# A two-layer hybrid decoder in one kernel: scaled rows and transposes for the norms, column blocks for the NSA compression

## The chip, the cores and the metric

One NeuronCore of a Trainium2 chip. The metric is the device time of one execution in microseconds (us). The kernel before was run three times: median 2697.93 us, from 2696.49 to 2704.11. The trace comes from a further, profiled execution.

## The reference, cut to what matters

Two layers, each a token mixer and a gated MLP, both between RMS norms with an adaptive shift, scale and gate. Sequence 256, width 2048, one batch, float32. Only what the change touches:

```python
h = rms_norm(x, norm_pre_mix[l]) * (1.0 + sc1) + sh1          # pre_norm; the same before the MLP
y = token_mixing(h, ...)                                      # four head groups, then w_out
x = x + g1 * rms_norm(y, norm_post_mix[l])

# inside token_mixing, each group's output is normalised: MLA, S5, NSA
o = concat([rms_norm(o_a, gn_mla), rms_norm(o_b, gn_s5), rms_norm(o_c, gn_nsa), o_d])

# NSA compression: 15 blocks of 32 rows, stride 16, of k and of v
h = gelu((xb + pos_emb).reshape(B, N, L * D) @ w1); k_cmp = h @ w2

# S5: a diagonal complex scan over time per group, 32 groups of 16 channels, 64 states
x_t = lam * x_{t-1} + B u_t ;  y_t = Re(C x_t) + d * u_t
```

MLA's two inputs (384 and 256 wide) have an RMS norm too.

## The kernel before, in words

Everything runs in one program that is written down once; a scheduler puts each engine's instructions into a fixed order by priorities, and the engines keep to it. Whatever waits holds up all that stands behind it on its engine.

**The weight stream.** The large products read float32 weight tiles of 128x1024 (`wload`, line 406, one transfer of 512 KB each). ScalarE rounds a tile to a high part `wh` (L423) and VectorE takes the rest `wl` (L424), both with raised priority; TensorE makes three products of each pair (`mm3`), named `mm<-ht,wh`, `mm<-ht,wl` and so on, where `ht` holds the split activations. Everything else that TensorE does goes into PSUM banks `mx` from two pools of two banks, "lanes" 0 and 1; with `lane = None` allocations alternate between the lanes. A bank is handed out in the order of the program, so a step that takes banks of a lane waits for the earlier step in that lane.

**Plain float32 products.** Products that don't go through the split stand in the trace as two weight loads and two matmuls each, one per pass. A transpose stands there once.

**pre_norm** (L577 on) runs three times: before the MLP of layer 0, before layer 1's mixer, before the MLP of layer 1. `residual` (L679) computes the row statistics on VectorE and builds two diagonal matrices, `set_diag` (L569; L573 on VectorE). `x` (two halves of 128 rows, `tt`) is updated in four column blocks `j` (L701), the first two before the products, the last two after the first part of pre_norm. TensorE multiplies each 128x128 block of `x` by the diagonal, which transposes and scales it at once (32 products per norm); ScalarE adds scale and shift (L597), and the result is split into `ht` (L599, L600). The first four of eight steps `k2` are written ahead of the weight stream, the rest between its tiles.

**norm_T** (L770) normalises a group's output that lies transposed: ScalarE squares it (L777), TensorE adds up the squares over partitions with a column of ones, one product for each 128 columns, VectorE computes the reciprocal root, TensorE spreads it over the partitions, VectorE applies it (L784). It runs five times per layer: S5, MLA q, MLA kv, MLA out, NSA out.

**nsa_compress** (L971) computes, for k and for v, `st` (18 columns: 16 blocks and two position vectors for each of 16 row offsets) times `w1`, which comes in four tiles `rawm` of 512 KB (two buffers, L454, moderate priority). All 16 products add up in the same 18 PSUM partitions of one bank, 256 columns wide. The sum is copied, transposed in two pieces, and goes through gelu and `w2`. It uses lane 1.

**s5** (L1537) uses lane 0 and works on four quarters (half, parity): eight products for `V` (64 rows of the array: the parity's half), the twists, scans and back-twists on VectorE (L1542, L1577), and twelve products for `y`, whose output goes to 64 partitions (again the parity's half). `s5_tables` prepares matrices, with products in blocks of 64 output partitions.

In `mixers` the order is: S5, the two token-major products (`gemm_a`), gates, `nsa_compress`, the remaining weight products for GDN, the two GDN halves in lockstep, one per lane, then MLA and NSA in lockstep, then `w_out`.

Of the kernel before, what the change touches and what calls it, by code (L numbers as in the profile page):

```python
# [12 lines left out]
F32 = mybir.dt.float32  # L13
# [3 lines left out]
AF = mybir.ActivationFunctionType  # L17
# [175 lines left out]
class Ker:  # L193
# [102 lines left out]
    def constants(self):  # L296
# [38 lines left out]
        self.diag = t([P, 2, P], F32, "diag")  # L335

        self.cm01 = t([P, 2, 32], F32, "cm01")
        self.cmadd = t([P, 2, 32], F32, "cmadd")
# [227 lines left out]
        self.rsqrt(v, y, self.sm(ss.shape[-1], "ra"))  # L566
        return y

    def set_diag(self, ss):  # L569

        r = self.rsqrt_cols(ss)
        for tt in range(2):
            i = self.nc.vector.tensor_scalar(self.diag[:, tt], self.ident, r[:, tt:tt + 1], 1.0 / RSC,  # L573
                                             op0=ALU.mult, op1=ALU.mult)
        return i

    def pre_norm(self, l, which):  # L577

        nc = self.nc
        for k2 in range(KT // 2):  # L580
            if k2 in (2, 4, 6):
                yield
            ps = self.mx()
            for i in range(2):
                k = 2 * k2 + i
                for tt in range(2):
                    self.mm(ps[:, i * 256 + tt * P:i * 256 + (tt + 1) * P], self.x[:, tt, k * P:(k + 1) * P],
                            self.diag[:, tt], True, True)
# [12 lines left out]
            if k2 == 0 and self.add_rest is not None:  # L601
                self.turn_ins = (i,) + self.turn_ins[1:]
                self.add_rest(i)
                self.add_rest = None

    def row_scale(self):
# [72 lines left out]
    def residual(self, sums, zs, done):  # L679

        nc = self.nc
        tot = self.small.tile([P, 3, 2], F32, name="bt", tag="bt", bufs=1)
        nc.vector.tensor_reduce(tot, sums, axis=AX.X, op=ALU.add)
        r = self.rsqrt_cols(tot[:, 0])
        sxx = self.x_stats()
        t = self.sm(2, "ct")
        for tt in range(2):
            nc.vector.scalar_tensor_tensor(t[:, tt:tt + 1], tot[:, 1, tt:tt + 1], r[:, tt:tt + 1], tot[:, 2, tt:tt + 1],
                                           op0=ALU.mult, op1=ALU.add)
        for tt in range(2):  # L690
            nc.vector.scalar_tensor_tensor(t[:, tt:tt + 1], t[:, tt:tt + 1], r[:, tt:tt + 1], sxx[:, tt:tt + 1],
                                           op0=ALU.mult, op1=ALU.add)
        d = self.set_diag(t)
# [9 lines left out]
        add(range(2), d)  # L703
        self.add_rest = lambda i: add(range(2, 4), i)

    def new_squares(self):
        with self.after(*self.norm_ins):
# [62 lines left out]
    def norm_T(self, scr, chunks, banks, n, gains, outs):  # L770

        nc = self.nc
        ss = self.mx(2)
        i, m = 0, 2 * len(chunks)
        for bi, (b, w) in enumerate(banks):
            sq = scr[:, bi % 2 * 512:bi % 2 * 512 + w]
            nc.scalar.activation(sq, b, AF.Square)  # L777
            for j in range(w // P):
                self.mm(ss[:, j % 2:j % 2 + 1], sq[:, j * P:(j + 1) * P], self.ones[:, 0:1], i == 0, i == m - 1)
                i += 1  # L780
# [192 lines left out]
    def nsa_compress(self, l, r, kvt, kT, kc, vb):  # L973
# [13 lines left out]
        for nm, src in (("k", kcT), ("v", vT)):  # L987
            w2 = r(P)
            nc.sync.dma_start(w2, I["nsa_w2_" + nm][l])
            st = r(16, 18)  # L990
            nc.vector.tensor_copy(st[:, :, 0:16], src.rearrange("p (m q) -> p q m", q=16))
            nc.vector.tensor_copy(st[:, :, 16:18], self.vs(l, "pos_" + nm).rearrange("p (q h) -> p q h", h=2))
            acc = self.mx(256)
            for q0 in range(0, 16, 4):
                raw = self.mload(I["nsa_w1_" + nm][l, q0 // 4])
                for q in range(4):
                    self.mm(acc[:18], st[:, q0 + q], raw[:, q * 256:(q + 1) * 256], q0 + q == 0, q0 + q == 15)
            ab = r(256)[:18]
            nc.scalar.copy(ab, acc[:18])
# [388 lines left out]
    def s5_tables(self, l, q, gs):  # L1388
# [97 lines left out]
        for half in range(2):  # L1486
# [2 lines left out]
            place(((bbr, bbi), (bbr, bbi)), half)  # L1489
            ps = self.mx(256).rearrange("p (q n) -> p q n", q=4)  # L1490
            for qd in range(4):
                for e in range(2):
                    for ri in range(2):
# [44 lines left out]
    def s5(self, l, r, Uc, oT):  # L1538
# [6 lines left out]
        t1, t2 = (wz[:, i * 516:(i + 1) * 516].rearrange("p (e n) -> p e n", e=4) for i in range(2))  # L1545
# [5 lines left out]
        a1, a2 = t1[:, :, 1:], t2[:, :, 1:]  # L1551
        for t in (t1, t2):
            nc.gpsimd.memset(t[:, :, 0:1], 0.0)
        for qr in range(4):

            half, par = qr // 2, qr % 2
            quads = range(4 * half, 4 * half + 4)
            o = 64 * par
            es = slice(8 * half + par, 8 * half + 8, 2)
            Er, Ei = E[:, 0, es], E[:, 1, es]  # L1560
            V = []
            for ri in range(2):
                ps = self.mx().rearrange("p (e n) -> p e n", e=4)
                for e, qd in enumerate(quads):
                    self.mm(ps[:, e], G[o:o + 64, qd, ri], Uc[o:o + 64, qd], True, True)
                V.append(ps)

            TTm(a1, V[0], Er, mul)
            TTm(a2, V[1], Ei, mul)
            TTm(zr, a1, a2, add)  # L1570
            TTm(a1, V[1], Er, mul)
            TTm(a2, V[0], Ei, mul)
            TTm(zi, a1, a2, sub)
            for z in (zr, zi):
                for e, qd in enumerate(quads):
                    d0 = self.s5m2[:, l, 2 * qd + par:2 * qd + par + 1].to_broadcast([P, P])
                    nc.vector.tensor_tensor_scan(z[:, e], d0, z[:, e], 0.0, mul, add)  # L1577
            TTm(a1, zr, Er, mul)
            TTm(a2, zi, Ei, mul)
            TTm(a1, a1, a2, sub)  # L1580
            TTm(zr, zr, Ei, mul)
            TTm(zi, zi, Er, mul)
            TTm(a2, zr, zi, add)
            y = self.mx().rearrange("p (q n) -> p q n", q=4)
            for e, qd in enumerate(quads):
                yy = y[o:o + 64, e]
                self.mm(yy, To[o:o + 64, qd], Uc[o:o + 64, qd], True, False)
                for ri, t in enumerate((t1, t2)):
                    self.mm(yy, H[:, 2 * qd + par, ri], t[:, e, 0:P], False, ri == 1)
            for h in range(2):  # L1590
                for s in range(2):
                    of = 64 * h + 32 * par
                    nc.scalar.activation(yv[of:of + 32, 2 * half:2 * half + 2, :, s], y[o + 32 * s:o + 32 * s + 32, h::2],  # L1593
                                         AF.Gelu_apprx_tanh)
# [33 lines left out]
    def mixers(self, l, first):  # L1628
# [301 lines left out]
```

## Time and profile before

| | |
|---|---|
| median of three runs | 2697.93 us |
| the profiled execution | 2690.51 us |
| its span, first to last instruction | 2688.7 us |
| TensorE busy | 96% of the span |
| VectorE busy | 71% |
| ScalarE busy | 47% |
| DMA, mean over the span | 231 GB/s |
| granted TensorE clock, mean | 0.977 |

A matmul's duration in the trace includes the time in which it travels through the array, and neighbours overlap in it. The time that it takes from its neighbours is the distance between two starts: of a row with n matmuls of one kind that took T in all, each lasting d, it is (T − d) / (n − 1).

### The profile page before, as it was taken

To read this page: it belongs to the slowest core of one execution; us is meant where nothing else is said; L and a number is where in the kernel's file an instruction comes from. 1 tells how busy PE (TensorE), PEld (TensorE's weight loads), DVE (VectorE), ACT (ScalarE), POOL (GpSimd) and SP (SyncE) were. 2 spreads that over 40 slices of the span, in tenths; PEclk is the share of its full clock that TensorE was granted. 3 is DMA by queue.
4 is the path that set the end of the run, shared out by engine and by line. 5 is a ranking of instruction groups with operands and counts; after the bars stand their busy time and mean duration, and the time that the engine had idled before them with its cause. 6 is when DMAs were issued, how large, how long until landed. Compare 5 with 4: busy or idle time off the path is not lost. (4 is left out here: it accounts for less than half of the span.)

```text
span 2688.7 us, 44484 instructions
## 1 busy us (share of the span) xinstructions
PE 2570.3 (96%) x17604; PEld 2285.4 (85%) x17604; DVE 1908.3 (71%) x3014; ACT 1260.1 (47%) x2004; POOL 10.2 (0%) x22
## 2 busy tenths in 40 slices
PE   7879999898999999999989999989899999999998
PEld 4568788677999999988868888978899999998886
DVE  5568888688787778766978889474777655555555
ACT  3344463556454444444545446454544444444443
POOL 0000000000000000000000000000000000000000
PEclk9979999898999999999999999999999999999999
DMA  8866666676888888866767578255587655555554
GB/s 344 313 209 200 227 239 231 233 277 222 292 284 288 292 290 293 287 228 235 249 220 239 165 251 274 98 193 173 191 278 275 206 187 181 183 185 186 184 189 148
DMA packets 171264, 620.89 MB, mean 231 GB/s; under 512 B 19440, under 2 KB 20272, under 8 KB 169520
## 3 DMA queue, kind: packets, MB, share of 16 engines
q1 hardware_dynamic: 170048, 617.00, 67.0%
q8 instruction: 138, 2.26, 0.3%
q10 hardware_dynamic: 1008, 1.06, 0.1%
q14 instruction: 70, 0.57, 0.1%
HBM read 613.75 MB, written 4.23 MB: 230 GB/s over the span
## 5 line engine op out<-in xcount | busy, mean ns | idle before, releaser
L228 PE MATMUL mm<-ht,wh 128*128 128x256 f32 x7168 | 1311.2, 283 | 6.8 <-ACT ht L423 5.8
L423 ACT CAST wh<-raw 128x1024 fp32r<-128x1024 f32 (+1 forms) x740 | 771.6, 1044 | 965.0 <-PE mm L228 792.1
L424 DVE TENSOR_TENSOR wl<-raw,wh 128x1024 fp32r<-128x1024 f32 (+1 forms) x740 | 895.9, 1213 | 380.2 <-ACT wh L423 377.1
L228 PEld LDWEIGHTS mm<-ht,wh 128*128 128x128 f32 x7168 | 1112.7, 189 | 22.9 <-issue 8.4
L228 PE MATMUL mm<-ht,wl 128*128 128x256 f32 x3584 | 1017.1, 284 | 2.7 <-DVE wl L424 2.7
L228 PEld LDWEIGHTS mm<-ht,wl 128*128 128x128 f32 x3584 | 674.5, 188 | 10.4 <-DVE wl L424 6.3
L228 PE MATMUL mm<-wh,ht 128*128 128x512 f32 (+1 forms) x1600 | 510.8, 396 | 8.6 <-DVE ry L256 3.9
L462 DVE SCALAR_TENSOR_TENSOR acc<-rawa,condc,acc 128x1024 f32<-128x1024 f32 x300 | 384.3, 1281 | 165.4 <-DMA rawa<-in_w_ada_dram 163.0
L228 PEld LDWEIGHTS mm<-wh,ht 128*128 128x128 f32 x1600 | 302.7, 190 | 73.2 <-ACT gth L1377 4.3
L228 PE MATMUL mm<-wl,ht 128*128 128x512 f32 (+1 forms) x800 | 317.2, 396 | 0.6 <-DVE wl L424 0.6
L228 PE MATMUL mx<-arena 128*128 128x128 f32 (+9 forms) x1576 | 228.1, 318 | 15.5 <-DVE gea L1151 9.7
L228 PE MATMUL mx<-wh,ht 128*128 128x512 f32 x704 | 222.3, 396 | 0.0
L228 PEld LDWEIGHTS mx<-arena 128*128 128x128 f32 (+5 forms) x1576 | 161.1, 168 | 59.0 <-issue 20.5
L228 PEld LDWEIGHTS mm<-wl,ht 128*128 128x128 f32 x800 | 152.4, 190 | 31.7 <-DVE wl L424 1.2
L228 PEld LDWEIGHTS mx<-wh,ht 128*128 128x128 f32 x704 | 132.6, 188 | 32.3
L228 PE MATMUL mx<-wl,ht 128*128 128x512 f32 x352 | 139.6, 397 | 0.0
L424 DVE TENSOR_TENSOR ht<-arena,ht 128x1024 fp32r<-128x1024 f32 x52 | 63.6, 1223 | 41.1 <-ACT ht L423 40.8
L1758 DVE SCALAR_TENSOR_TENSOR arena<-mm,vec,arena 128x255 f32<-128x255 f32 (+1 forms) x176 | 78.3, 476 | 6.7 <-ACT arena L1756 5.8
L423 ACT CAST ht<-arena 128x1024 fp32r<-128x1024 f32 x52 | 54.2, 1050 | 56.7 <-PE mm L228 31.3
L228 PEld LDWEIGHTS mx<-wl,ht 128*128 128x128 f32 x352 | 66.3, 188 | 16.5 <-DVE wl L424 0.3
L232 PE MATMUL mx<-ident,arena 128*128 128x128 f32 (+1 forms) x328 | 59.4, 292 | 21.5 <-ACT arena L826 13.7
L232 PEld LDWEIGHTS mx<-ident,arena 128*128 128x128 f32 (+1 forms) x328 | 39.5, 147 | 40.2 <-ACT arena L826 17.4
(314 smaller groups left out, 1520.4 us busy)
## 6 DMA issues: line engine op xcount, KB each, us to landing
raw<-in_ffn_w_in_dram SPq DMA_DIRECT2D x352, 512.0 KB, 4.2
rawa<-in_w_ada_dram SPq DMA_DIRECT2D x330, 512.0 KB, 5.1
raw<-in_ffn_w_out_dram SPq DMA_DIRECT2D x176, 512.0 KB, 4.3
raw<-in_w_in_dram SPq DMA_DIRECT2D x116, 512.0 KB, 4.5
raw<-in_w_out_dram SPq DMA_DIRECT2D x64, 512.0 KB, 4.3
arena<-in_w_ada_dram SPq DMA_DIRECT2D x36, 512.0 KB, 8.0
raw<-in_w_in_dram SPq DMA_DIRECT2D x32, 426.0 KB, 4.0
rawm<-in_w_ada_dram SPq DMA_DIRECT2D x9, 512.0 KB, 9.6
```

Source lines behind the costliest of these rows:

```text
L228: self.nc.tensor.matmul(out, lhsT=lhsT, rhs=rhs, start=start, stop=stop)
L232: self.nc.tensor.transpose(out, in_, self.ident[:k, :k])
L423: self.nc.scalar.copy(hi.bitcast(F32R), src)
L424: self.last_lo = self.nc.vector.tensor_sub(lo.bitcast(F32R), src, hi)
L462: self.nc.vector.scalar_tensor_tensor(acc, w, self.condc[:, kc:kc + 1], acc, op0=ALU.mult, op1=ALU.add)
L1758: nc.vector.scalar_tensor_tensor(c[:, s:], ps[m][:, :256 - s], self.fconv(l, 2 - s, f), c[:, s:], op0=ALU.mult, op1=ALU.add)
```

## The change

**pre_norm**: `set_scale` leaves the row factors in a small tile `rs`. Each quarter of `x` (512 columns) is multiplied by `rs` into a scratch area, the first quarter on VectorE, the other three on ScalarE, and TensorE transposes the scaled blocks. Only block 0 of `x` is updated before the first scaling, block 1 after it, blocks 2 and 3 as before.

**norm_T**: all banks are squared side by side; VectorE adds the squares down to 256 columns; two products with the ones remain.

**nsa_compress**: `st` is widened to 32 columns, filled with zeros on GpSimd first. Of the four offsets in a weight tile, each has its own 32 output partitions. The four partial sums in 128 partitions are added and transposed in one by four small products with `ident2` (two stacked identities).

**s5**: a half's two parities are written together, with V products alternating between the halves of the array's rows and y products between the halves of its columns; four V banks, two y banks; `lane = None`. A second pair of `t` buffers lies in columns that `nsa_compress` uses too. In `s5_tables` two loops are exchanged.

```diff
-    def set_diag(self, ss):
+    def set_scale(self, ss):
         r = self.rsqrt_cols(ss)
-        for tt in range(2):
-            i = self.nc.vector.tensor_scalar(self.diag[:, tt], self.ident, r[:, tt:tt + 1], 1.0 / RSC, ...)
-        return i
+        self.rs = self.sm(2, "rs")
+        return self.nc.vector.tensor_scalar(self.rs, r, 1.0 / RSC, None, op0=ALU.mult)
     def pre_norm(self, l, which):
+        slots = (AT[0:4] if which else (AT[7], AT[8], AT[4], AT[5]) if l else (AT[9], AT[10]))
         for k2 in range(KT // 2):
+            if k2 % 2 == 0:
+                q = k2 // 2
+                xs = self.reg(slots[q % len(slots)], 1024)(2, 512)
+                for tt in range(2):
+                    src = self.x[:, tt, q * 512:(q + 1) * 512]
+                    if q:
+                        nc.scalar.activation(xs[:, tt], src, AF.Identity, scale=self.rs[:, tt:tt + 1])
+                    else:
+                        i = nc.vector.tensor_scalar(xs[:, tt], src, self.rs[:, tt:tt + 1], None, op0=ALU.mult)
+                if q == 0 and self.add_rest is not None:
+                    self.add_rest[0](i)
...
-                    self.mm(ps[...], self.x[:, tt, k * P:(k + 1) * P], self.diag[:, tt], True, True)
+                    self.tp(ps[...], xs[:, tt, k * P:(k + 1) * P])
     def norm_T(self, scr, chunks, banks, n, gains, outs):
-        for bi, (b, w) in enumerate(banks):
-            sq = scr[:, bi % 2 * 512:bi % 2 * 512 + w]
-            nc.scalar.activation(sq, b, AF.Square)
-            for j in range(w // P):
-                self.mm(ss[:, j % 2:j % 2 + 1], sq[:, j * P:(j + 1) * P], self.ones[:, 0:1], i == 0, i == m - 1)
+        for b, w in banks:
+            nc.scalar.activation(scr[:, o:o + w], b, AF.Square)
+            o += w
+        sq = scr[:, 0:256]
+        if o == 1024:
+            nc.vector.tensor_tensor(scr[:, 0:512], scr[:, 0:512], scr[:, 512:1024], op=ALU.add)
+            o = 512
+        for i in range(256, o, 256):
+            nc.vector.tensor_tensor(sq, sq, scr[:, i:i + 256], op=ALU.add)
+        for j in range(2):
+            self.mm(ss[:, j:j + 1], sq[:, j * P:(j + 1) * P], self.ones[:, 0:1], True, True)
     def nsa_compress(...):
-                    self.mm(acc[:18], st[:, q0 + q], raw[...], q0 + q == 0, q0 + q == 15)
+                    self.mm(acc[32 * q:32 * q + 32], st[:, q0 + q], raw[...], q0 == 0, q0 == 12)
-                self.tp(psT[:, i * 32:i * 32 + 18], ab[:, i * P:(i + 1) * P])
+                for j in range(2):
+                    self.mm(psT[:, i * 32:i * 32 + 32], ab[:, i * P:(i + 1) * P], self.ident2[:, 32 * j:32 * j + 32], j == 0, j == 1)
     def s5(...):
-        for qr in range(4):
-            half, par = qr // 2, qr % 2
+        wt = (wz, self.reg(A_OT + 1024, 1032)(1032))
+        for half in range(2):
+            V = [[view(self.mx()) for _ in range(2)] for _ in range(2)]
...
+                    for par in range(2):
+                        self.mm(V[par][ri][:, e], G[o:o + 64, qd, ri], Uc[o:o + 64, qd], True, True)
     def mixers(...):
+        self.lane = None
+        self.s5(l, r5, Uc, oT["s5"])
         self.lane = 0
-        self.s5(l, r5, Uc, oT["s5"])
```

How the order moves, at three places. Rows are instructions of one engine in its fixed order; a number after `mx_` names the PSUM bank's allocation, xN that N like it follow each other; one row's product stands for two matmuls in the trace where it isn't split.

TensorE, layer 1's compression of k; before, with `mx_14817` the sum, `mx_14349` and `mx_14368` S5's last outputs and its gate:

```order
L228 MATMUL mm<-ht,wh 128x256
L228 MATMUL mx_14817<-rawm,arena 18x256 x4
L228 MATMUL mx_14349<-arena 64x128
L228 MATMUL mx_14817<-rawm,arena 18x256
L228 MATMUL mx_14368<-arena 128x256 x2
L228 MATMUL mx_14817<-rawm,arena 18x256 x3
L228 MATMUL mm<-ht,wh 128x256
```

Now, with `mx_14824` the sum; 25 weight products stand between its first row and the second, 9 between the second and the third:

```order
L228 MATMUL mx_14824<-rawm,arena 32x256 x8
L228 MATMUL mm<-ht,wl 128x256
...
L228 MATMUL mx_14824<-rawm,arena 32x256 x4
L228 MATMUL mm<-ht,wh 128x256 x2
...
L228 MATMUL mx_14824<-rawm,arena 32x256 x4
...
L228 MATMUL mx_14850<-ident_126,arena 128x32 x4
```

The compression no longer stands between S5's products but behind them: from S5's last y product to the last compression product of v there were 44 weight products in layer 1 and 85 in layer 0, and now there are 349 and 275. The four offsets of a tile stand next to each other.

TensorE at the turn into the MLP of layer 0; before, with the four banks of `k2` 0 to 3:

```order
L228 MATMUL mx_5524<-diag,arena 128x128
L228 MATMUL mx_5540<-diag,arena 128x128
L228 MATMUL mx_5524<-diag,arena 128x128 x3
L228 MATMUL mx_5540<-diag,arena 128x128 x3
L228 MATMUL mx_5550<-diag,arena 128x128 x4
L228 MATMUL mx_5560<-diag,arena 128x128 x4
L228 MATMUL mm<-ht,wh 128x256 x2
```

Now:

```order
L232 MATMUL mx_5518<-ident,arena 128x128 x4
L232 MATMUL mx_5534<-ident,arena 128x128 x4
L232 MATMUL mx_5546<-ident,arena 128x128
L232 MATMUL mx_5556<-ident,arena 128x128
L228 MATMUL mm<-ht,wh 128x256 x3
```

The remaining six transposes of `k2` 2 and 3 stand twelve weight products further on, no longer ahead of the stream. On ScalarE the first scaling of quarter 1 stands ahead of the scale-and-shift of `k2` 0.

TensorE, S5 in layer 1, the V products of the first half, banks 14188 and 14189 for parity 0, 14190 and 14191 for parity 1:

```order
L228 MATMUL mx_14188<-arena 128x128
L228 MATMUL mx_14190<-arena 128x128
L228 MATMUL mx_14188<-arena 128x128
L228 MATMUL mx_14189<-arena 128x128
L228 MATMUL mx_14191<-arena 128x128
L228 MATMUL mx_14190<-arena 128x128
```

and of a y bank, as before:

```order
L228 MATMUL mx_14248<-arena 64x128 x10
```

V alternates here; in layer 0 and in the second half mostly three or four of one bank follow each other. The y products of one parity follow each other in a row of ten, as before.

## Rows read from the trace of the kernel before

**Rows 1.** The page's first part: busy time, share of the span, instructions.
```profile
PE 2570.3 (96%) x17604; PEld 2285.4 (85%) x17604; DVE 1908.3 (71%) x3014; ACT 1260.1 (47%) x2004; POOL 10.2 (0%) x22
```
**Rows 2.** Stretches: length, busy time per engine (count), PEclk, DMA share, GB/s.
```profile
612.00:631.00 19.00, 6.68 (x54) 6.61 (x55) 17.22 (x58) 7.42 (x16) 0.00 (x0) 0.64 0.27 89
...
1480.00:1550.00 70.00, 69.32 (x419) 56.09 (x417) 61.90 (x124) 30.98 (x49) 0.00 (x0) 1.00 0.51 164
1550.00:1600.00 50.00, 49.79 (x346) 39.70 (x345) 38.56 (x72) 20.31 (x37) 0.00 (x0) 1.00 0.70 239
```
**Rows 3.** Timeline, TensorE, layer 1's compression: start, length, instruction.
```profile
1570.50 1.05 PE L228 MATMUL mx<-ones,arena 128*128 128x1 f32 x8
1571.48 1.90 PE L228 MATMUL mx<-rawm,arena 128*18 128x256 f32 x8
...
1573.65 0.40 PE L228 MATMUL mm<-ht,wh 128*128 128x256 f32 x2
1573.89 0.28 PE L228 MATMUL mm<-ht,wl 128*128 128x256 f32 x1
```
**Rows 4.** TensorE by line and form: busy us, mean ns, idle before.
```profile
L232 PE MATMUL mx<-ident,arena 128*128 128x128 f32 x320 | 58.2, 293 | 21.5 <-ACT arena L826 13.7 <-ACT arena L1199 2.9 <-ACT arena L1483 1.9
...
L228 PE MATMUL mx<-rawm,arena 128*18 128x256 f32 x128 | 31.5, 381 | 0.1
...
L228 PE MATMUL mx<-ones,arena 128*128 128x1 f32 x168 | 20.9, 245 | 0.9 <-ACT arena L777 0.8
L228 PE MATMUL mx<-arena 64*128 64x128 f32 x128 | 19.6, 290 | 3.1 <-ACT arena L1619 2.7
```
**Rows 5.** Timeline, TensorE, a modulation product in four column blocks of 32.
```profile
103.86 0.62 PE L228 MATMUL mx<-acc,arena 128*32 128x512 f32 x1
103.86 0.63 PE L228 MATMUL mx<-arena 128*32 128x512 f32 x3
104.31 0.59 PE L228 MATMUL mx<-acc,arena 128*32 128x512 f32 x1
104.32 1.46 PE L228 MATMUL mx<-arena 128*32 128x512 f32 x9
```
**Rows 6.** The tile rawm, 1540 to 1600 us: its transfers from issue to landing.
```profile
DMA to landing us min/median/max: 3.4/4.1/6.1
```
**Rows 7.** VectorE and ScalarE lines: ns min/median/max, first and last start, forms.
```profile
L600 DVE TENSOR_TENSOR ht<-hf,ht x27: 424/682/693, 628.2 to 1935.9; 128x512 fp32r<-128x512 f32 x21, 128x256 fp32r<-128x256 f32 x6
...
L460 DVE TENSOR_SCALAR acc<-rawa,condc x20: 722/746/754, 158.5 to 2005.1; 128x1024 f32<-128x1024 f32 x20
...
L616 ACT ACTIVATE arena<-arena x8: 613/629/631, 8.7 to 18.9; 128x512 f32<-128x512 f32 x8
```
**Rows 8.** Timeline, layer 1, the end of MLA and NSA.
```profile
1803.93 1.95 PE L228 MATMUL mx<-ones,arena 128*128 128x1 f32 x16 [0.60 <-ACT arena L777]
...
1817.93 0.60 PE L232 MATMUL mx<-ident,arena 128*128 128x128 f32 x4
```
**Rows 9.** Timeline, the turn into the MLP of layer 0.
```profile
623.55 0.48 DVE L573 TENSOR_SCALAR diag<-ident,cy 128x128 f32<-128x128 f32 x2
623.95 2.73 DVE L701 SCALAR_TENSOR_TENSOR arena<-arena,cy 128x512 f32<-128x512 f32 x4
...
624.75 5.76 PE L228 MATMUL mx<-diag,arena 128*128 128x128 f32 x32 [4.95 <-DVE arena L701]
627.28 1.02 ACT L597 ACTIVATE hf<-mx,mod 128x256 f32<-128x256 f32 x2 [9.10 <-PE mx L228]
...
630.26 0.48 PE L228 MATMUL mm<-ht,wh 128*128 128x256 f32 x2
...
633.69 1.05 PE L228 MATMUL mx<-diag,arena 128*128 128x128 f32 x8
```
**Rows 10.** Stretches within that turn, columns as in rows 2.
```profile
624.70:628.80 4.10, 4.05 (x19) 4.05 (x20) 2.86 (x6) 1.25 (x3) 0.00 (x0) 0.50 0.01 4
628.80:640.00 11.20, 11.20 (x97) 11.20 (x97) 11.17 (x16) 9.63 (x17) 0.00 (x0) 1.00 0.37 125
```

More of the change, by code (lines that the diff above doesn't have):

```diff
@@ L602, in pre_norm @@
                 self.turn_ins = (i,) + self.turn_ins[1:]
-                self.add_rest(i)
+                self.add_rest[1](i)
                 self.add_rest = None
@@ L701, in add @@
                         nc.vector.scalar_tensor_tensor(xs, zs[j][tt], r[:, tt:tt + 1], xs, op0=ALU.mult, op1=ALU.add)
-        add(range(2), d)
-        self.add_rest = lambda i: add(range(2, 4), i)
+        add(range(1), d)
+        self.add_rest = [lambda i: add(range(1, 2), i), lambda i: add(range(2, 4), i)]
     def new_squares(self):
@@ L989, in nsa_compress @@
             nc.sync.dma_start(w2, I["nsa_w2_" + nm][l])
-            st = r(16, 18)
+            st = r(16, 32)
+            nc.gpsimd.memset(st, 0.0)
             nc.vector.tensor_copy(st[:, :, 0:16], src.rearrange("p (m q) -> p q m", q=16))
@@ L996, in nsa_compress @@
                 for q in range(4):
-                    self.mm(acc[:18], st[:, q0 + q], raw[:, q * 256:(q + 1) * 256], q0 + q == 0, q0 + q == 15)
-            ab = r(256)[:18]
-            nc.scalar.copy(ab, acc[:18])
+                    self.mm(acc[32 * q:32 * q + 32], st[:, q0 + q], raw[:, q * 256:(q + 1) * 256], q0 == 0, q0 == 12)
+            ab = r(256)
+            nc.scalar.copy(ab, acc)
             psT = self.mx()
             for i in range(2):
-                self.tp(psT[:, i * 32:i * 32 + 18], ab[:, i * P:(i + 1) * P])
+                for j in range(2):
+                    self.mm(psT[:, i * 32:i * 32 + 32], ab[:, i * P:(i + 1) * P], self.ident2[:, 32 * j:32 * j + 32],
+                            j == 0, j == 1)
             a = r(2, 18)
@@ L1491, in s5_tables @@
             for qd in range(4):
-                for e in range(2):
-                    for ri in range(2):
+                for ri in range(2):
+                    for e in range(2):
                         pe = 2 * qd + e
@@ L1544, in s5 @@
         wz = r(2056)
-        t1, t2 = (wz[:, i * 516:(i + 1) * 516].rearrange("p (e n) -> p e n", e=4) for i in range(2))
+        wt = (wz, self.reg(A_OT + 1024, 1032)(1032))
+        ts = [[w[:, i * 516:(i + 1) * 516].rearrange("p (e n) -> p e n", e=4) for i in range(2)] for w in wt]
         zr, zi = (wz[:, 1032 + i * 512:1032 + (i + 1) * 512].rearrange("p (e n) -> p e n", e=4) for i in range(2))
@@ L1550, in s5 @@
         nc.sync.dma_start(glu.rearrange("p k n -> p (k n)"), I["s5_w_glu"][l])
-        a1, a2 = t1[:, :, 1:], t2[:, :, 1:]
-        for t in (t1, t2):
+        for t in itertools.chain(*ts):
             nc.gpsimd.memset(t[:, :, 0:1], 0.0)
-        for qr in range(4):
-            half, par = qr // 2, qr % 2
+        view = lambda ps: ps.rearrange("p (e n) -> p e n", e=4)
+        for half in range(2):
             quads = range(4 * half, 4 * half + 4)
[L1558 to L1561, printed above, removed]
+            V = [[view(self.mx()) for _ in range(2)] for _ in range(2)]
@@ L1562, in s5 @@
             for ri in range(2):
-                ps = self.mx().rearrange("p (e n) -> p e n", e=4)
                 for e, qd in enumerate(quads):
[L1565 to L1584, printed above, removed]
-            for e, qd in enumerate(quads):
[L1586 to L1594, printed above, removed]
+                    for par in range(2):
+                        o = 64 * par
+                        self.mm(V[par][ri][:, e], G[o:o + 64, qd, ri], Uc[o:o + 64, qd], True, True)
+            for par in range(2):
+                es = slice(8 * half + par, 8 * half + 8, 2)
+                Er, Ei = E[:, 0, es], E[:, 1, es]
+                Vr, Vi = V[par]
+                a1, a2 = (t[:, :, 1:] for t in ts[par])
+                TTm(a1, Vr, Er, mul)
+                TTm(a2, Vi, Ei, mul)
+                TTm(zr, a1, a2, add)
+                TTm(a1, Vi, Er, mul)
+                TTm(a2, Vr, Ei, mul)
+                TTm(zi, a1, a2, sub)
+                for z in (zr, zi):
+                    for e, qd in enumerate(quads):
+                        d0 = self.s5m2[:, l, 2 * qd + par:2 * qd + par + 1].to_broadcast([P, P])
+                        nc.vector.tensor_tensor_scan(z[:, e], d0, z[:, e], 0.0, mul, add)
+                TTm(a1, zr, Er, mul)
+                TTm(a2, zi, Ei, mul)
+                TTm(a1, a1, a2, sub)
+                TTm(zr, zr, Ei, mul)
+                TTm(zi, zi, Er, mul)
+                TTm(a2, zr, zi, add)
@@ new lines, in s5 @@
+            y = [view(self.mx()) for _ in range(2)]
+            for e, qd in enumerate(quads):
+                for par in range(2):
+                    o = 64 * par
+                    self.mm(y[par][o:o + 64, e], To[o:o + 64, qd], Uc[o:o + 64, qd], True, False)
+                for ri in range(2):
+                    for par in range(2):
+                        o = 64 * par
+                        self.mm(y[par][o:o + 64, e], H[:, 2 * qd + par, ri], ts[par][ri][:, e, 0:P], False, ri == 1)
@@ L1595, in s5 @@
+            for par in range(2):
+                o = 64 * par
+                for h in range(2):
+                    for s in range(2):
+                        of = 64 * h + 32 * par
+                        nc.scalar.activation(yv[of:of + 32, 2 * half:2 * half + 2, :, s],
+                                             y[par][o + 32 * s:o + 32 * s + 32, h::2], AF.Gelu_apprx_tanh)
         yg = Uc.rearrange("p q m -> p (q m)").rearrange("p (c t) -> p c t", c=4)
```

13 lines of the change are left out of this document (4 added, 9 removed).

## The prediction
> **What bounds the kernel now.** I read the page's first part first: TensorE is busy 96% of the span, VectorE 71%, ScalarE 47% [rows 1]. A share over the span says little, so the table of stretches came next. In layer 1's mixers, around S5 and the compression, TensorE is busy 69.32 of 70 and 49.79 of 50 us, at full clock; VectorE has 61.90 and 38.56 us there [rows 2]. So TensorE decides in these stretches, with VectorE close behind while S5 runs (88%) and far behind (77%) where the compression stands. The stretch 612 to 631 is different: TensorE 6.68 of 19 us, VectorE 17.22, PEclk 0.64 [rows 2]. There the row statistics decide, and TensorE waits. The change takes work from TensorE almost everywhere, and from the statistics' chain next to nothing. So what goes from TensorE in the first kind of stretch counts in full, as long as VectorE, a transfer or a chain doesn't take over.
>
> **The change part by part.** Distances between starts are used, not durations.
>
> *Compression.* 64 products, 128 matmuls [rows 4]. Eight in a row take 1.90 us at 0.38 each, so one takes (1.90 − 0.38)/7 = 0.217 us from its neighbours, 27.8 us in all [rows 3, 4]. The form that replaces them stands in the trace: four products of 32 columns start 0.01 us apart, the next four 0.45 us later, the rest 0.43 us apart, the time that one such product of 512 columns needs by itself [rows 5]. Four blocks thus cost what one does; at 256 columns 128/4 × 0.217 = 6.9 us. That removes 20.8 us. Added: for each of four sums the transposing products, 8 matmuls in place of 2 transposes. A product with a full set of weights and few columns takes (1.05 − 0.25)/7 = 0.114 us [rows 3, 4], a transpose (0.60 − 0.29)/3 = 0.10 us [rows 4, 8]: 8 × 0.114 − 2 × 0.10 = 0.7 us, four times, +2.9 us. The zeros for `st` are GpSimd's, which is idle; the second lies behind S5's last read of `t`, as does all of k's compression, because of the shared columns.
>
> The weight tiles are a new wait. Two are loaded ahead; the next two are sent when the first two are read and land 4.1 us later (3.4 to 6.1) [rows 6]. Before, a tile's own products took 1.7 us. Now the order leaves 25 weight products of 0.12 us each (two from 1573.65 to 1573.89 [rows 3]), 3 us, before the third tile of k in layer 1: about 1.2 us of waiting, behind which the weight stream is queued. I take that for each of four sums, +4.8 us; the ends are nothing and 6.1 − 3 = 3.1 us four times, 12.4 us.
>
> *norm_T.* Per layer the norms have 8 + 6 + 4 + 8 + 8 = 34 products, 68 matmuls, and keep 20; in both layers 96 go, 96 × 0.114 = −10.9 us [rows 3, 4]. Added on VectorE: 0.68 us for 512 columns and 0.42 for 256 [rows 7], 4.6 us per layer. Where TensorE is the bound this is hidden. At the end of MLA and NSA it isn't: TensorE waits there for ScalarE's squares [rows 8]. After the last square there now come 0.68 + 0.42 us of sums and 4 products instead of 8 or more: +0.6 us for each of two norms in two layers, +2.4 us. Sum −8.5 us, ends −10.9 and −4.
>
> *Transposes in pre_norm.* The 16 products of each norm that lie within the weight stream take two matmuls of (1.05 − 0.28)/7 = 0.11 us (the row of eight [rows 9]) and become one transpose of 0.10 to 0.11: 48 × 0.115 = −5.5 us. ScalarE scales 18 blocks of 512 columns at about 0.63 us [rows 7], 11 us on an engine that is busy for half the span.
>
> *The turns.* Before: two diagonals at 623.55, updates of `x` from 623.95 at 2.73/4 = 0.68 us, 32 matmuls from 624.75 to 630.26, the first 4.1 us at half clock, and only then the weight stream; the first scale-and-shift stood at 627.28 [rows 9, 10]. Now: one small instruction, so updates start 0.25 us earlier, two of them end at 625.1; two scalings on VectorE, between 0.37 us (half of the 0.75 that 1024 columns take) and 0.75 [rows 7], I take 0.4, the nearest form: 625.9; four transposes at half clock, 0.9 us and the way through the array, 627; ScalarE first does its own scaling, until 627.3, then scale-and-shift and VectorE's two splits; the stream starts near 628.3 instead of 630.26. Six transposes then lie inside it, and its first products run at half clock. Of the 2 us I keep 1, three times: −3 us. VectorE, nearly full there, gains 0.5 to 1.2 us of work; if it decides, a turn is 1.2 us longer. Ends −6 and +3.6 us.
>
> *S5.* The y products go on in rows of ten of one parity, so there I take nothing. V alternates in one half of layer 1, 32 matmuls out of 128 [rows 4] at 0.11 us; if they pair, −1.8 us. For the tables' exchanged loops I take next to nothing, since most of layer 0's lie before TensorE is the bound; with V −2 us in all, ends −4 and 0. Against this stands cover: before, the compression filled part of TensorE's time while VectorE worked on S5; now S5 has the weight stream alone beside it, each tile of which needs VectorE too. VectorE was at 88% [rows 2]. I allow +4 us, ends 0 and +12.
>
> Sum: −20.8 + 2.9 + 4.8 − 8.5 − 5.5 − 3 − 2 + 4 = −28.1 us. The profiled execution took 2690.5 us, so 2662.4 by the sum; it lies 7.4 us below the median of the runs shown, so for a median 2697.9 − 28.1 = about 2670 us.
>
> A rule of the Trainium skill speaks against the turns. The rows show TensorE at half clock while it had only the first diagonal products, and at full clock from 628.8 on [rows 10]; no row has such a turn with transposes alone. The page "TensorE: Matmul & The Clock Gate", section "Part 4: PE-mode transpose", says that transposes don't count as work for the clock. By it the turns would give nothing or lose, as the third rival has it.
>
> **The rivals.**
>
> 1. *VectorE takes over in S5.* For it: 88% [rows 2], and the stream is the only cover. Against: with the compression behind S5, the stretch behind it is as much lighter for VectorE. If 6 us per layer are lost instead of 2, and the norms' adds weigh at their upper end, −28 + 8 + 4.5 = −15: 2683 us.
>
> 2. *The compression's loads decide; slower than before.* Place: the tiles of `w1` after the first two of each layer, 12 of them, with two buffers and one load queue that the weight stream shares. Each costs TensorE its landing time less the cover. At 4.1 us and 3 us of cover, and two tiles sent together, it is in the sum. If each of the 12 came singly, 3.1 us late [rows 6], that is 37 us in place of 4.8: −28 + 32 = +4 on the sum; with the profiled execution's 2690.5 and the same step to the median, 2702 us. It decides from 2.8 us per tile on. Against: the queue's busy share is 0.5 to 0.7 there [rows 2].
>
> 3. *The clock at the turns.* If only weight products bring the clock back, the 4.1 us at half clock [rows 10] are spent on the stream: 2 us of work lost per turn, 6 us, −22: 2676 us.
>
> 4. *The blocks don't run side by side,* because in the compression each product has new weights and its own columns of `w1`. For it: nothing; in rows 5 each product has its own weights and data too. The 20.8 us would stay: −28 + 21 − 4.8 = −12, 2686 us.
>
> **How the numbers follow.** A measurement of this kernel tells about 0.3%, 8 us, from no change. My forecast, with a range of its own of 2655 to 2684: 0.60. First rival 0.15, second 0.07, third 0.08, fourth 0.05; 0.05 is left for more than the sum, where shorter waits in GDN and attention add to it, around 2645. The range takes in the first and third rivals and most of the fourth: 2650 to 2690; outside are the second and the best cases, 0.12. Faster by over 0.3%, below 2690: the forecast, the third, the best cases and 0.08 of the first and fourth, whose times lie just below that bound, 0.81. Within 0.3%: the rest of these two, 0.12. Slower: the second, 0.07.
>
> **What would show it.** The 128 matmuls of 18 columns should be 128 of 32 columns that start in fours 0.01 us apart, and take 7 to 9 us in all; the ones products should be 72 instead of 168. The first weight product should come about 4.6 us after the first update of `x`, not 6.3 [rows 9]. Wrong would be: gaps on TensorE released by `rawm`, beyond 5 us in all; VectorE over 95% in S5 with TensorE waiting for `wl`; PEclk below 0.64 in the turns.

## The result: faster, and the profile after

The changed kernel takes 2667.34 us (median of four runs, 2664.41 to 2668.30); the kernel before, in four runs of the same series, 2699.35. The ratio is 0.9885 [0.9867, 0.9903], 31 us faster by it (the medians lie 32 apart). Forecast were 2670 us and −28.1 us. The profiled execution took 2664.41 us with a span of 2662.4, against 2690.51 and 2688.7 before.

The page's first part, to be read against [rows 1]:

```profile
PE 2524.5 (95%) x17436; PEld 2251.5 (85%) x17436; DVE 1918.8 (72%) x3035; ACT 1264.9 (48%) x2018; POOL 12.6 (0%) x30
```

TensorE by line and form (busy us, mean ns | idle before and its releasers), the counterpart of [rows 4]:

```profile
L232 PE MATMUL mx<-ident,arena 128*128 128x128 f32 x416 | 75.7, 299 | 40.9 <-DVE arena L590 22.4 <-ACT arena L840 12.1 <-ACT arena L1501 2.1
...
L228 PE MATMUL mx<-arena 64*128 64x128 f32 x128 | 16.7, 291 | 3.9 <-ACT arena L1644 3.7
...
L228 PE MATMUL mx<-rawm,arena 128*32 128x256 f32 x128 | 10.0, 404 | 2.2 <-DMA rawm<-in_nsa_w_k_dram 2.1
L228 PE MATMUL mx<-ones,arena 128*128 128x1 f32 x72 | 9.8, 247 | 4.1 <-DVE asm L835 2.4 <-DVE amx L823 1.6
...
L228 PE MATMUL mx<-ident,arena 128*128 128x32 f32 x32 | 4.2, 274 | 0.0
```

The compression's 128 matmuls keep TensorE busy for 10.0 us, before 31.5, where the prediction named 7 to 9; the wait for `rawm` is 2.1 us; the ones products are 72 and 9.8 us, before 168 and 20.9. The V products of S5 (64 rows of the array, 128 columns) went from 19.6 to 16.7.

Timeline of TensorE, layer 0's compression (start, length):

```profile
292.46 1.07 PE L228 MATMUL mx<-rawm,arena 128*32 128x256 f32 x16
```

Two tiles of `w1` in 1.07 us. In [rows 3] one tile took 1.90. The trace has the 16 starts of this row in four groups of four: 0.007 us apart within a group, and a new group each 0.215 us.

The three stretches of [rows 2] (length, busy time per engine, PEclk, DMA share, GB/s):

```profile
612.00:631.00 19.00, 7.77 (x63) 7.03 (x64) 17.88 (x57) 8.28 (x16) 0.00 (x0) 0.61 0.20 72
1480.00:1550.00 70.00, 68.38 (x446) 58.88 (x444) 59.49 (x116) 32.25 (x51) 0.53 (x1) 1.00 0.51 160
1550.00:1600.00 50.00, 49.92 (x442) 44.96 (x441) 43.45 (x91) 26.53 (x59) 0.00 (x0) 1.00 0.82 270
```

S5 no longer fills the second of them: layer 1's scans, which started between 1475.4 and 1546.9 us before, now start between 1466.1 and 1524.0. The stretch that holds them now:

```profile
1466.00:1526.00 60.00, 58.38 (x345) 48.81 (x344) 53.13 (x90) 21.44 (x33) 0.00 (x0) 1.00 0.53 162
```

VectorE is busy for 53.13 of 60 us there, 89%, as much as before (88%), and TensorE for 97%. In the third stretch the DMA share is up from 0.70 to 0.82; it holds another part of the weight stream now. In the first, PEclk is 0.61, below the 0.64 that the prediction named as a sign of being wrong: half clock lasts from 609.9 to 627.0 us, before from 615.2 to 628.8. Yet the turn got shorter, because TensorE spends most of that time waiting for the row statistics (busy 7.77 of 19 us).

Timeline of the turn into layer 0's MLP, against [rows 9], and the stretches ahead of and behind the moment at which the clock comes back, against [rows 10]:

```profile
621.70 0.17 DVE L572 TENSOR_SCALAR rs<-cy 128x2 f32<-128x2 f32 x1
621.78 1.41 DVE L710 SCALAR_TENSOR_TENSOR arena<-arena,cy 128x512 f32<-128x512 f32 x2
623.10 0.88 DVE L590 TENSOR_SCALAR arena<-arena,rs 128x512 f32<-128x512 f32 x2
...
623.64 2.58 PE L232 MATMUL mx<-ident,arena 128*128 128x128 f32 x10 [5.28 <-DVE arena L590]
...
624.68 0.72 ACT L588 ACTIVATE arena<-arena,rs 128x512 f32<-128x512 f32 x1 [10.72 <-DVE arena L710]
625.30 1.91 ACT L606 ACTIVATE hf<-mx,mod 128x256 f32<-128x256 f32 x4
...
626.23 0.97 PE L228 MATMUL mm<-ht,wh 128*128 128x256 f32 x3
```

```profile
621.00:627.00 6.00, 3.34 (x13) 2.67 (x14) 5.32 (x18) 2.32 (x5) 0.00 (x0) 0.50 0.00 1
627.00:640.00 13.00, 13.00 (x109) 12.78 (x108) 13.00 (x17) 12.49 (x22) 0.00 (x0) 1.00 0.47 162
```

The first weight product comes 4.45 us after the first update of `x`; before it was 6.31, and 4.6 was forecast.

**Where the 26 us between the two traces lie.** The first update of `x` at each turn is a mark that every kernel has:

| first update of `x` | turn 1 | turn 2 | turn 3 |
|---|---|---|---|
| before | 623.95 | 1410.64 | 1911.53 |
| after | 621.78 | 1406.61 | 1887.38 |
| difference | −2.2 | −4.0 | −24.2 |

These are two single traces; the kernel before, run 29 times in one series, took between 2687 and 2703 us. Layer 1's mixers give some 20 us, and layer 0's mixers only 2, though the same products went from both. Most of what the compression, the norms and S5 should have given in layer 0 isn't there, and yet the sum came out right. The experiments ask for both.

### The profile page after: what moved, and what is told of

Same layout as the page of the kernel before. It is cut to its first block, busy times and chain, and to the rows that moved or that the text cites. A ratio compares the mean times of both kernels' runs of the same rounds, so it can differ in the third digit from the quotient of the medians.

```text
span 2662.4 us, 44182 instructions
## 1 busy us (share of the span) xinstructions
PE 2524.5 (95%) x17436; PEld 2251.5 (85%) x17436; DVE 1918.8 (72%) x3035; ACT 1264.9 (48%) x2018; POOL 12.6 (0%) x30
## 4 chain that ended last, share of the span: by engine, by line
PE 78%; DVE 9%; DMA 7%; ACT 4%; issue 2%; SPq 0%; ACTq 0%; DVEq 0%
PE mm L228 60%; PE mx L228 17%; DMA rawa<-in_w_ada_dram 5%; DVE wl L423 2%; DVE acc L461 2%; PE mx L232 1%; ACT wh L422 1%; DVE arena L1532 1%; ACT junk L669 0%; DVE arena L1207 0%; DMA rawm<-in_nsa_w_k_dram 0%; DMA arena<-in_w_ada_dram 0%; DVE arena L1412 0%; DMA vec<-in_vec_dram 0%; DVE arena L710 0%
## 5 line engine op out<-in xcount | busy, mean ns | idle before, releaser
L228 PEld LDWEIGHTS mm<-ht,wl 128*128 128x128 f32 x3584 | 676.0, 189 | 10.1 <-DVE wl L423 5.8
L228 PE MATMUL mx<-arena 128*128 128x128 f32 (+9 forms) x1576 | 221.6, 315 | 20.3 <-DVE gea L1169 10.2
L232 PE MATMUL mx<-ident,arena 128*128 128x128 f32 x416 | 75.7, 299 | 40.9 <-DVE arena L590 22.4
L232 PEld LDWEIGHTS mx<-ident,arena 128*128 128x128 f32 x416 | 51.3, 150 | 60.4 <-issue 19.3
```

The costliest lines, as they stand in the source:

```text
L228: self.nc.tensor.matmul(out, lhsT=lhsT, rhs=rhs, start=start, stop=stop)
L232: self.nc.tensor.transpose(out, in_, self.ident[:k, :k])
```

## The experiments

### One part at a time

Four kernels, each the kernel before with one part of the change, word for word as in the diff:

```diff
c_only: nsa_compress
+ self.mm(acc[32 * q:32 * q + 32], st[:, q0 + q], raw[...], q0 == 0, q0 == 12)
n_only: norm_T
+ nc.vector.tensor_tensor(sq, sq, scr[:, i:i + 256], op=ALU.add)
p_only: set_scale, pre_norm, residual
+ self.tp(ps[...], xs[:, tt, k * P:(k + 1) * P])
s_only: s5, s5_tables, lane = None around it
+ V = [[view(self.mx()) for _ in range(2)] for _ in range(2)]
```

> Only the compression in column blocks, all else as before. My sum: -20.8 for the blocks, +2.9 for the transposing products, up to +4.8 for tiles of w1 that come late, so -13 (ratio 0.995) with the waits and -18 (0.993) without them; the 128 products take about 10 us on TensorE instead of 31.5, and the gain stands at the end of both layers' mixers in like parts. Rival, the w1 tiles decide: gaps released by rawm of more than 10 us, and -8 or less. Rival, layer 0 has another bound: the gain is there behind the compression in layer 0 but gone again by the end of its mixers, and only layer 1's half, -7 to -9, is left.

> Only the squares added on VectorE before the products with the ones, all else as before. My sum: -10.9 on TensorE, +2.4 at the end of MLA and NSA, so -8.5 us (0.997). Rival, the sums lie in the way: before S5's norm and at the end of MLA and NSA TensorE waits for VectorE's adds, the gain falls below -4 (0.9985).

> Only scaled rows and transposes in place of diagonal products, all else as before. My sum: -5.5 within the weight stream and -1 for each of three turns, so -8.5 us (0.997). Rival, the clock: if transposes alone leave the clock at half in the turns, each loses 2 us and the whole is near -2.5 (0.999). Rival, VectorE and ScalarE decide the turns: nothing at the turns, -5 us or less in all.

> Only S5's pairs, its tables and the lanes, all else as before. My sum: -2 for products that pair, +4 for the cover that leaves S5, so +2 us (1.001). Rival, VectorE takes over in S5 and the compression behind it stands alone: +6 to +12 us (1.002 to 1.0045). Rival, the whole change's gain beyond my sum comes from here (fewer waits between the quarters): -4 us or more (0.9985).

Measured, with the kernel before at 2695.91 us; the third column follows from the ratio:

| part | ratio | us | my sum |
|---|---|---|---|
| compression | 0.9971 [0.9955, 0.9987] | −8 | −13 |
| norms | 0.9977 [0.9963, 0.9991] | −6 | −8.5 |
| scaled rows | 0.9933 [0.9913, 0.9953] | −18 | −8.5 |
| S5 | 0.9978 [0.9963, 0.9994] | −6 | +2 |

Two of four are off: the scaled rows give twice their count, and S5 gains where I had it lose. The compression is below its sum, but in its trace the products take 11.8 us, near the 10 expected, and the waits for `rawm` are 1.1 us:

```profile
L228 PE MATMUL mx<-rawm,arena 128*32 128x256 f32 x128 | 11.8, 388 | 1.1 <-DMA rawm<-in_nsa_w_k_dram 1.1
```

So its loads don't decide. The other rival of that run came true: the first update of `x` at turn 1 stands at 623.96, as before (623.95), and only layer 1's mixers, from turn 2 to turn 3, are shorter, by 8.1 us. In layer 0 the gain is gone by the end of its mixers.

A view in which the kernels with and without scaled rows differ is VectorE's waits between 1400 and 1500 us, the start of layer 1's mixer (us in total, times, longest). Before, p_only, and the whole change:

```profile
DVE acc L462 <- DMA rawa<-in_w_ada_dram: 9.8, 3, 4.6
```

```profile
DVE acc L461 <- DMA rawa<-in_w_ada_dram: 1.5, 1, 1.5
```

```profile
DVE acc L461 <- DMA rawa<-in_w_ada_dram: 0.5, 2, 0.3
```

`rawa` holds the modulation's weights, whose tiles are loaded and summed up on VectorE beside the mixers, 96 in layer 0 and 64 in layer 1. A late one stops VectorE, and the splits of the weight stream behind it. VectorE's timeline before shows one of them (the wait in brackets):

```profile
1443.22 1.22 DVE L424 TENSOR_TENSOR wl<-raw,wh 128x1024 fp32r<-128x1024 f32 x1 [0.24 <-ACT wh L423]
1448.78 2.60 DVE L462 SCALAR_TENSOR_TENSOR acc<-rawa,condc,acc 128x1024 f32<-128x1024 f32 x2 [4.33 <-DMA rawa<-in_w_ada_dram]
1451.30 2.35 DVE L424 TENSOR_TENSOR wl<-raw,wh 128x1024 fp32r<-128x1024 f32 x2
```

TensorE waits 1.9 us for the `wl` behind it. Nothing in the scaled rows shortens such a load; they only shift the instructions around it. Of p_only's lead on the kernel before, some 4 us arise here: 3.7 us at layer 1's first weight product, 7.6 at S5's first scan. The whole change wins 2.5 us at this place (6.8, then 9.3), so a part of its 20 us in layer 1 may be the modulation's too.

### The same without the modulation's tiles

To take that out, the light kernels load and sum one of 16 tiles beside the mixers:

```diff
             if kc:
                 yield
+            if kc and not self.paced:
+                continue
             w = self.rawa.tile([P, 1024], F32, name="rawa", tag="rawa")
```

> The kernel before, with 15 of each 16 tiles of the modulation weights left out, and their sums on VectorE, for the blocks that run beside the mixers (not those beside the MLPs, so that part of the modulation is wrong). It is the base for the next two, which leave out the same. In the mixers VectorE no longer waits for rawa, and TensorE's half-clock stretches between 430 and 560 us should shrink: well faster than before, 20 to 60 us.

> The same left out, with the scaled rows and transposes alone. Theory: half of that part's -19 us came from a chance, that a late tile of the modulation weights no longer stopped VectorE at the start of layer 1's mixer (0.5 to 1.5 us of such waits there against 8 to 11 without the part). Then it should now be 8.5 us, my sum's amount, ahead of the light kernel before, 6 to 11. Rival, the part itself gains more than its count (in the turns or the stream): 15 us or more here too.

> The same left out, and the compression in column blocks alone. My sum: -18 without waits for w1 tiles, -13 with 4.8 us of them; alone, with the modulation, it measured -8. Theory: layer 0's half is kept here, so -13 to -18, ratio 0.9735 to 0.9755. Rival: the count of the compression is itself too high, -8 again, 0.9775.

> The kernel before with the same modulation tiles left out as in the light kernel before (ratio 0.9804 to the kernel before), and S5's part alone. My sum said +2 us with the cover lost. Alone, with the modulation, it measured -6. If that is S5's own gain (the parities of a half no longer wait for each other's banks), it stays at -5 to -10 here, ratio 0.977 to 0.9785; if it was a chance of the modulation's waits, it is -2 to +4, 0.980 to 0.982.

> The same left out, with the whole change. Theory: in layer 0 most of what TensorE saves by 430 us, some 12 us, is lost again by 560 us to waits that hang on the modulation's tiles; without them it should stay, so the whole is 30 to 45 us ahead of the light kernel before, and in layer 0 the turn into the MLP starts 10 us or more earlier. Rival, layer 0's loss is in the chains of the attention groups themselves: 25 us or less, and the turn of layer 0 starts 2 to 5 us earlier as now.

| kernel | median us (range) | ratio to the kernel before | against before_light |
|---|---|---|---|
| before_light | 2642.46 (2639.84 to 2643.65) | 0.9804 [0.9779, 0.9830] | |
| p_light | 2634.82 (2630.37 to 2638.86) | 0.9777 [0.9753, 0.9800] | −7.6 |
| c_light | 2626.68 (2625.66 to 2627.86) | 0.9743 [0.9725, 0.9760] | −15.8 |
| s_light | 2637.29 (2636.48 to 2642.22) | 0.9786 [0.9767, 0.9804] | −5.2 |
| after_light | 2605.32 (2601.94 to 2612.78) | 0.9674 [0.9647, 0.9701] | −37.1 |

c_light and s_light ran in another series than the rest; the kernel before had 2695.44 us there and 2694.96 here. The norms weren't run light; the remainder for them is −37.1 + 7.6 + 15.8 + 5.2 = −8.5.

Leaving the tiles out gives 52 us by itself, within the range expected. Without the modulation the scaled rows give 7.6 us (8.5 in my sum), the compression 15.8 (between the 13 with and the 18 without waits), the norms' remainder 8.5 (8.5). The −18 of p_only fell by more than half: some 10 us of it hang on the modulation, as expected; between the same two marks of layer 1 its lead doesn't grow here (2.0, then 1.6 us). S5's gain stayed, though the ranges of s_light and before_light overlap. As the norms weren't run, that their remainder equals their count agrees with parts that add up, but doesn't test it.

The stretch 430 to 560 us, layer 0's GDN, MLA and NSA, in the kernels before, after, before_light and after_light (columns as above):

```profile
430.00:560.00 130.00, 113.05 (x649) 93.98 (x648) 102.20 (x248) 66.18 (x150) 3.23 (x3) 0.92 0.70 238
```

```profile
430.00:560.00 130.00, 107.96 (x559) 87.05 (x558) 107.47 (x259) 67.23 (x155) 3.23 (x3) 0.87 0.70 246
```

```profile
430.00:560.00 130.00, 128.48 (x743) 107.46 (x742) 77.40 (x201) 78.64 (x172) 3.23 (x3) 1.00 0.45 149
```

```profile
430.00:560.00 130.00, 128.30 (x727) 105.96 (x726) 80.63 (x192) 81.56 (x174) 3.26 (x3) 1.00 0.47 154
```

In the first two TensorE is idle for 17 and 22 us and its granted clock averages 0.92 and 0.87, which is 20 and 34 us at half clock; in the light ones, which hold later work there (turn 1 comes 31 and 41 us earlier), it is busy throughout, at 1.00. The change has freed TensorE of work ahead of the stretch, so it comes to it earlier: the last 64x64 product of GDN starts at 409.1 us before and at 399.0 after. It then waits longer, and more of its work runs at half clock: VectorE reads the first result of `w_out` at 560.0 and 554.7, so 5.3 of the 10.1 us are left. Without the modulation the gain gets through, 8.1 us at the first of these marks and 11.4 at the second: the first update of `x` at turn 1 moved from 592.57 to 581.00, 11.6 us, against 2.2 with it; at turn 2 from 1379.41 to 1364.26, at turn 3 from 1862.20 to 1824.91. Layer 0's loss hangs on the modulation, then, and not on the attention groups' own chains.

What of the modulation does it isn't shown, as the light kernels leave out loads and sums at once. VectorE's waits for its tiles in this stretch, before and after:

```profile
DVE acc L462 <- DMA rawa<-in_w_ada_dram: 12.0, 10, 3.7
```

```profile
DVE acc L461 <- DMA rawa<-in_w_ada_dram: 9.8, 10, 2.5
```

They got shorter while TensorE's idle time grew, so late tiles alone don't explain the loss; the sums on VectorE, some 40 us of the 130 in both, are the rival that is left.

### S5 left as before

```diff
-        self.lane = None
+        self.lane = 0
         self.s5(l, r5, Uc, oT["s5"])
-        self.lane = 0
```

with `s5` and `s5_tables` as before, and the other three parts.

> The change without S5's part (that as before, lanes too). If S5's part gains by itself what it gained alone, -6 us, this is 6 us behind the whole change, 2674 or a ratio of 0.991. If that gain was got from the compression's old place beside S5, or if S5 has lost the cover that I allowed 4 us for, it is as fast as the whole change or faster, 0.987 to 0.989.

Measured 2677.52 us, ratio 0.9937 [0.9915, 0.9959], 17 us faster than before. The whole change is 14 us ahead of it by the ratios, 10 by the medians, which come from two series; so S5's part gives no less here than the 6 us that it gave alone, and the rival, that it needed the compression's old place or lost its cover, falls. The three parts alone add up to −32 by the table above; together they give −17. In its trace the first update at turn 1 comes at 632.53, 8.6 us later than before, and the stretch 430 to 560 has 101.46 us of TensorE at a clock of 0.86. So beside the modulation the parts don't add up.

What S5's part does by itself: TensorE's timeline in s_light shows V products of alternating halves, twelve matmuls in 0.94 us:

```profile
174.57 0.94 PE L228 MATMUL mx<-arena 64*128 64x128 f32 x12
```

They start in pairs, the two of a pair 0.007 us apart and one pair each 0.11 us, so 0.06 us go to each, where in a row of one half they take 0.11. And VectorE's first twists, which wait for V, in before and s_only (idle before them, and on what):

```profile
L1542 DVE TENSOR_TENSOR arena<-mx,arena 128x512 f32<-128x512 f32 x32 | 21.5, 686 | 8.2 <-PE mx L228 8.1
```

```profile
L1542 DVE TENSOR_TENSOR arena<-mx,arena 128x512 f32<-128x512 f32 x32 | 21.1, 685 | 3.5 <-PE mx L228 3.4
```

The V products of both parities are ready when VectorE turns to the second. Layer 0's last scan starts 22 us earlier for it (at 279.2 before, at 256.9 in s_only and at 257.3 in the changed kernel). The pairs save TensorE some 3 us (V products 19.6 us before, 17.1 in s_only; 18.7 in before_light, 15.0 in s_light); where the rest of S5's gain comes from isn't shown.

### Two attempts at the modulation

The first sends more of layer 0's modulation early, the second takes its arithmetic from VectorE, both on top of the whole change:

```diff
after_rate:
-        bg = ((((0, (4, 5, 8, 6, 9, 7)),), (0.5, 0.6, 1, 0.8)), ...
+        bg = ((((0, (4, 5, 8, 6, 9, 7)),), (0.7, 0.7, 0.8, 0.8)), ...
after_pool, in ada_mac:
+        if not self.paced:
+            self.nc.gpsimd.tensor_scalar(w if kc else acc, w, self.condc[:, kc:kc + 1], None, op0=ALU.mult)
+            if kc:
+                self.nc.gpsimd.tensor_tensor(acc, acc, w, op=ALU.add)
```

> The whole change, with layer 0's modulation sent earlier: 0.7 tiles per weight tile instead of 0.5 up to the GDN halves, 0.7 instead of 0.6 in them, 0.8 instead of 1 in MLA and NSA. If layer 0's loss between 430 and 560 us comes from the modulation tiles that are left for that stretch, the time is 3 to 8 us below the whole change, ratio 0.986 or less. Rival: VectorE, at about 90% around S5 in layer 0, now decides there, and the time is the same or up to 10 us longer, 0.989 to 0.993.

> The whole change, with the modulation's scaling and adding beside the mixers on GpSimd, two instructions per tile, in place of one of 1.2 us on VectorE. If the wait of VectorE for a late tile, behind which the weight halves stand, is what costs layer 0 its gain, 10 us or more go from the whole change, ratio 0.985 or less. Rival: GpSimd needs so long per tile (over 3.5 us for the pair, 96 tiles in layer 0's 330 us) that the rest is drained ahead of the output product, 20 us or more longer, ratio above 0.995.

after_rate: 2697.28 us, 1.0005 [0.9992, 1.0018]. The whole gain is gone, three times what the rival allowed. The sums in the stretch 430 to 580 us, in the changed kernel and in this one:

```profile
L461 DVE SCALAR_TENSOR_TENSOR acc<-rawa,condc,acc 128x1024 f32<-128x1024 f32 x37 | 47.3, 1280 | 11.7 <-DMA rawa<-in_w_ada_dram 11.7
```

```profile
L461 DVE SCALAR_TENSOR_TENSOR acc<-rawa,condc,acc 128x1024 f32<-128x1024 f32 x45 | 57.6, 1281 | 13.1 <-DMA rawa<-in_w_ada_dram 12.8
```

The edit did the reverse of what it was for: by 430 us three more tiles were summed, but between 430 and 580 eight more than in the changed kernel, tiles that used to come later. Turn 1 came 7.2 us later, and in 430 to 560 TensorE was busy for 91.58 us at a clock of 0.83:

```profile
430.00:560.00 130.00, 91.58 (x484) 74.33 (x483) 105.31 (x281) 57.25 (x142) 3.26 (x3) 0.83 0.68 236
```

That agrees in sign with the theory but isn't a test of early sending. Another 17 us went between turns 2 and 3, in layer 1's mixers, whose rates weren't touched. Half clock lasts 31 us there instead of 10; what started it is open.

after_pool: 2912.29 us, 1.0799 [1.0779, 1.0818]. The rival came true, and costs far more than its 20 us; GpSimd's instructions of the pair, busy us and mean ns:

```profile
L459 POOL TENSOR_SCALAR rawa<-rawa,condc 128x1024 f32<-128x1024 f32 x150 | 477.3, 3182 | 74.7 <-DMA rawa<-in_w_ada_dram 74.6
L461 POOL TENSOR_TENSOR acc<-acc,rawa 128x1024 f32<-128x1024 f32 x150 | 375.0, 2500 | 12.4
```

5.7 us a tile against 1.28 on VectorE. So this tells nothing about VectorE's stall. No version that was run beats the whole change.

## Why the prediction was right, and where it was not

**The bottleneck.** In layer 1's mixers, where TensorE is the bound, what was taken from it counted, and more: some 20 us. The sum took it as counting in layer 0 too, and from 430 us on that was wrong. The table of stretches that I read had none of layer 0's mixers; one for 430 to 560 would have shown 113.05 of 130 us at 0.92.

**Compression, −20.8 + 2.9 + 4.8.** Blocks run side by side: 10.0 us busy. A group of four takes 0.215 us, so the 32 groups take 6.9 us, as counted; the 10.0 also hold the time in which the last group of each row runs out. (The formula for one matmul's time doesn't fit here, because starts within a group lie close together.) The waits for `rawm` are 2.1 us, not 4.8, so the second rival falls: its 12 late tiles would have been 37 us. The sum was −13.1; light it measures −15.8, and alone beside the modulation −8.

**norm_T, −8.5.** 72 matmuls, as counted; −6 alone, with an interval from −2 to −10. The −8.5 in the light kernels is a remainder and not a measurement, so this term agrees and isn't shown.

**Transposes and turns, −5.5 and −3.** −7.6 light. The turn of layer 0 is 1.9 us shorter up to its first weight product, where I had allowed 1. Up to the hundredth weight matmul, the transposes and the products at half clock among them included, the three turns are 2.3, 1.5 and 2.2 us shorter. That alone this part measures −18 is for the larger part not its own doing.

**The third rival, the clock.** It doesn't decide: all three turns got shorter, and the 2 us lost per turn didn't appear. After the change the clock was back 3.4, 3.5 and 4.0 us after the first transpose of the three turns, 0.8 to 1.5 us after the first weight product; in p_only 4.4, 3.9 and 6.2 us after the first transpose, 1.4 to 3.7 after the first weight product; before, with diagonal products, 4.1, 5.8 and 3.3 us after the first of them, each time ahead of the weight stream. The ranges overlap. The rule of the Trainium skill's page "TensorE: Matmul & The Clock Gate", "Part 4: PE-mode transpose", that transposes don't count, is neither needed for these rows nor excluded by them.

**S5, −2 + 4.** This is the term that failed, in sign: the pairs gave more (19.6 to 16.7 us in this trace), and the +4 for lost cover was for nothing, since VectorE's own waits for V shrank from 8.1 to 2.6 us and S5 ended earlier. Light it measures −5.2 instead of +2 (the medians; the ranges overlap), alone −6 with an interval that excludes a loss. The first rival, VectorE as the bound in S5, falls with it: 89% busy, as before, with TensorE at 97%.

**The sum.** −28.1 forecast, −31 measured: that it fits so well is luck. Split over the layers, with half of the compression, the norms and S5 in each, the sum has −9.8 us in layer 0's mixers and −12.6 from turn 2 to turn 3, where a third of the transposes and turns comes in. The traces have −2.2 and −20.2, so the errors, 7.6 us each, cancel. The light kernels give −37, 9 more than the sum, most of it from S5 (7) and the compression (3); by their marks it lies in layer 1's mixers (−22.1), hardly in layer 0's (−11.6), and why isn't shown. The modulation takes 6 back on balance, mostly in layer 0. The prediction had neither in it.

## What to carry to other kernels

Work that is taken from the bound engine counted here only up to the next stretch where something else was late; a mark that all kernels have, at each stage's end, shows within one trace where a gain is lost. When parts alone don't add up to the whole, look for a shared background (here the modulation's loads and sums) whose waits move with every edit, and measure the parts once more without it. A shift of a background's rate moves its load somewhere: count where it lands before running it.

## What the runs showed of the hardware

- Four products with their own weights, data and 32 output partitions each run side by side at 256 float32 columns: groups of four matmuls start 0.215 us apart, as single ones did before (0.217). Two products that use different halves of the rows pair too, 0.06 us a matmul for 0.11.
- GpSimd needs 3.18 us to scale 128x1024 float32 values and 2.50 to add them to others; VectorE does both in one instruction of 1.28.
- In layer 0's mixers the loss goes together with the granted clock, 0.92 before, 0.87 after, 0.83 with more tiles in the stretch, 1.00 without them. Work at half clock takes longer: in the turn before, 19 diagonal matmuls took 4.05 us at half clock [rows 10], 0.21 each, against 0.11 at full.
